# A two-layer trunk on one core: the order in which the down and output projections load their blocks

## The chip, the core and the metric

The kernel runs on one core of a Trainium2 chip. The core has a matrix engine (TensorE, PE in the profile; its weight loads are PEld), three engines for elementwise work (VectorE or DVE, ScalarE or ACT, GpSimd or POOL), and SyncE (SP), which here does nothing but issue transfers. ACT and POOL issue some transfers too. Each has a queue of instructions of its own. The metric is the time of one execution on the device in microseconds (us); lower is better.

## The reference, cut to what matters

A trunk of two layers over a sequence of 1024 rows of width 1024, all in float32. Each layer has a mixer, a layer norm, a convolutional feed-forward part and a second layer norm:

```python
for i in range(DEPTH):                      # DEPTH = 2
    ...
    y = mixers[i % N_MIXERS](x * (1.0 + sc1) + sh1)
    x = layer_norm(DN_ALPHA * x + (1.0 + g1) * y, ln_g[i, 0], ln_b[i, 0])
    y = conv_ffn(x * (1.0 + sc2) + sh2, ffn_up[i], ffn_conv_w[i], ffn_conv_b[i], ffn_down[i])
    x = layer_norm(DN_ALPHA * x + (1.0 + g2) * y, ln_g[i, 1], ln_b[i, 1])
```

Layer 0's mixer is a gated delta net, layer 1's is retention. The two that are never reached are left out. The change touches two matrix products:

```python
def conv_ffn(h, w_up, conv_w, conv_b, w_down):
    ...
    return (jax.nn.silu(gate) * up) @ w_down          # 1024 x 2816 by 2816 x 1024, once per layer
def retention(h, w_in, w_out):
    ...
    return o.astype(h.dtype) @ w_out                   # 1024 x 2048 by 2048 x 1024, layer 1
```

## The kernel before, in words

**Precision.** Every float32 operand of a large product is split in two parts of a reduced format, a high and a low one: `split` (line 88) copies the block into the high part on ACT and subtracts it on DVE for the low part. A product of two blocks is then three matmuls (low by high, high by low, high by high), lines 278 to 280 in `mma`.

**The projections.** `proj_gen` (line 1265) computes the down projection of each layer and the output projection of retention. It cuts the rows, the columns and the inner dimension into halves and uses a Strassen-Winograd scheme with seven block products instead of eight. The seven are listed in `prods` (line 1419); each names an activation operand (`11`, `12`, `22`, `S1` to `S4`), a weight operand (`11`, `21`, `22`, `T1` to `T4`) and a function that merges the result. A product has `nj` steps, 11 in the down projections and 8 in the output projection, so a projection has 77 or 56 steps. A step multiplies one activation block of 128x512 with one weight block of 128x512 into four PSUM banks: twelve matmuls.

**What a step loads.** The activation blocks were combined earlier (the sums S1 to S4 included) and stored in DRAM, `ad` for the down projections and `od` for the output projection; `ablk` (made by `ablk_of`, line 1258) takes a buffer called `ar` from the tag `qkv` and loads one of them on SP's queue (line 1261). The weight blocks are loaded by `load_b` (line 1284, the transfer on line 1294) and combined on the fly by `bblk` on DVE (lines 1302, 1305, 1307). The blocks `11` and `T2` stay for later products (`Bw`; line 1294 writes them to the tag in `slots`), the others are short-lived (`Br`, tag `qkv`). The operand `22` needs no load of its own: it is the block kept for `T2`. `ops` (line 1312) does one step: it loads the activation block, combines the weight block and splits both.

**Buffers.** The tag `qkv` has 24 buffers of 128x512. In the down projections the `ar`, the `Br` and, in eleven of them, the blocks of `T2` share them. In the output projection they are shared with the split values of the retention (`vv`, two buffers for each chunk of 128 rows of a head). The targets of the splits (`ab`, `bb`) come from other tags, except in the last steps.

**Order.** Three loops run over product, step and row group. `ahead = 3` (line 1424): three weight blocks are loaded before the first step, and step n, after its own activation block, loads the weight block of step n+3, with `after("a")` queueing it behind the last activation load. The rows that the down projection also needs are fetched in the same loop: `gain_half` (line 1335) loads a half row group `xg` behind the last load of a block, POOL multiplies and adds to it, and it is stored again; `xload` (line 1344) and `load_row` (line 269) load the residual rows `xt`, also behind the last block's load.

The output projection is interleaved by hand with the retention: `run` (line 647) draws from generators by their due times, and `gate(j)` (line 1434) holds back step j of the first two products until the retention has written the activation blocks of its head. `take` and `give` keep account of the buffers of `qkv` in this interleaving; 20 of the 24 are in that account.

What the program says is not yet the order of the queues. At compile time a scheduler plays the program through in a model of time, hands out the buffers of a tag in program order as they come free, and lays down the order of each engine's queue; an instruction is queued when its operands and its buffer are ready in that model. Edges such as those of `after` are kept. On the chip the queues then run in that fixed order.

Of the kernel before, what the change touches and what calls it, by code (L numbers as in the profile page):

```python
# [33 lines left out]
def trunk_kernel(ctx: ExitStack, tc, A):  # L34
# [14 lines left out]
    def two(tag, dt=F32, name=None):  # L49
        if tag in ("qkv", "auh"):  # L50
            return tl(tag, [P, HALF], dt, name), tl(tag, [P, HALF], dt, name)
        t = tl(tag, [P, 2, HALF], dt, name)
        return t[:, 0], t[:, 1]
# [13 lines left out]
    def acc4():  # L67
        return [acc_tile(), acc_tile(), acc_tile(), acc_tile()]
# [19 lines left out]
    def split(dst_h, dst_l, src, eng=dve):  # L88
        act.activation(dst_h, src, AF.Copy)  # L89
        eng.tensor_tensor(dst_l, src, dst_h, ALU.subtract)  # L90
# [3 lines left out]
    def after(key):  # L94
        return tc.issue_after(anchor[key].ins) if key in anchor else nullcontext()
# [23 lines left out]
    def bg_step(tile=mm_tile):  # L119
        bg_ps[0] = tile  # L120
        if bg:
            bg.pop(0)()
# [38 lines left out]
    for k in range(KT):  # L161
        w = two("hTa", F32, "mvw")
# [113 lines left out]
    def mma(acc, t, a, w, first, last, mm):  # L276
        sl = slice(t * P, (t + 1) * P)
        mm(acc, a[1][:, sl], w[0], start=first, stop=False)  # L278
        mm(acc, a[0][:, sl], w[1], start=False, stop=False)  # L279
        mm(acc, a[0][:, sl], w[0], start=False, stop=last)  # L280
# [108 lines left out]
    def ln_hooks(half, xts, tag, vecs2, out, dst, key, npool=0):  # L389
        def build(f):  # L390
            out.append(build_one(tag, xts, *vecs2(), f, pool if f < npool else dve))
        return ([lambda f=f: build(f) for f in range(KT)]
                + [lambda t=t: ln_store(half, t, xts, dst, key) for t in range(4)])
# [297 lines left out]
    def take(tag, n):  # L691
        while free[tag] < n:
            yield lambda: free[tag] >= n
        free[tag] -= n

    def give(tag, n):
        free[tag] += n
# [567 lines left out]
    def proj_gen(nj, ablk, wsrc, slots, xsrc, G, final, ln_next, tag, ltags, dst, key, mm=pe.matmul, gate=None, gain=None):  # L1265
# [18 lines left out]
        def load_b(bn, j):  # L1284
            if bn not in src:
                return
            if bn == "11":
                t = C[j] = keep("c", j)
            elif bn == "T2":
                t = X[j] = keep("x", j)  # L1290
            else:
                t = R[bn, j] = tl("qkv", [P, HALF], name="Br")
            m = src[bn]
            anchor["w"] = sp.dma_start(t, wsrc[(m[1] == "2") * 1, j][:, hs((m[0] == "2") * 1)])

        def bblk(bn, j):
            if bn in ("11", "22"):
                return {"11": C, "22": X}[bn][j]
            if bn == "21":
                return R[bn, j]  # L1300
            if bn == "T1":
                dve.tensor_tensor(C[j], R[bn, j], C[j], ALU.subtract)
                return C[j]
            if bn == "T2":
                dve.tensor_tensor(C[j], X[j], C[j], ALU.subtract)
                return C[j]
            dve.tensor_tensor(R[bn, j], C[j], R[bn, j], ALU.subtract)  # L1307
            return R[bn, j]

        nst = [0]  # L1310

        def ops(an, bn, j, early):
            ra, rb = ablk(an, j), bblk(bn, j)
            n = nst[0]
            nst[0] += 1
            last = an == "22"
            at = ltags[0] if last and j >= nj - ltags[3] else ("wl", "hTb", "wr")[n % 3] if early else ("wl", "wr")[n % 2]
            wt = ltags[1] if last and j >= nj - ltags[2] else ("wh", "hTb", "hTb")[n % 3] if early else "wh"
            a = two(at, F32R, "ab")
            split(a[0], a[1], ra, pool if j < bal[an] else dve)  # L1320
            w = two(wt, F32R, "bb")
            split(w[0], w[1], rb, pool if j < bal["w" + bn] else dve)
            return a, w
# [3 lines left out]
        def acc_next():  # L1327
            nacc[0] += 1
            return sc_tile() if nacc[0] % 6 in (5, 0) else acc_tile()
# [5 lines left out]
        def gain_half(n):  # L1335
            hf, rs = n // 4, slice(HALF + n % 4 * P, HALF + (n % 4 + 1) * P)
            x = tl("lane", [P, HALF], name="xg")
            with after("w"):
                sp.dma_start(x, gain[1][rs, hs(hf)])
            for r, op in zip(grows, (ALU.mult, ALU.add)):  # L1340
                pool.tensor_tensor(x, x, r[hf], op)
            pool.dma_start(xsrc[rs, hs(hf)], x)

        def xload(half, t):
            xt = load_row(xsrc if half or not gain else gain[1], half, t)
            if half == 0 and gain:
                for r, op in zip(grows, (ALU.mult, ALU.add)):
                    for hf in range(2):
                        pool.tensor_tensor(xt[:, hs(hf)], xt[:, hs(hf)], r[hf], op)
            xts[half].append(xt)  # L1350
            stats[half].append(tl("st", [P, 2, 6]))

        def finish(half, t, nh, c):
            dve.tensor_tensor(c, c, G[nh], ALU.mult)  # L1354
            xv = xts[half][t][:, hs(nh)]
            dve.scalar_tensor_tensor(xv, xv, ALPHA, c, ALU.mult, ALU.add)  # L1356
            dve.bn_stats(stats[half][t][:, nh], xv)  # L1357
# [55 lines left out]
        def f4(t, acc):  # L1413
# [5 lines left out]
        prods = [("11", "11", f1), ("12", "21", f2), ("S1", "T1", f5), ("S2", "T2", f6), ("S4", "22", f3),  # L1419
                 ("S3", "T3", f7), ("22", "T4", f4)]  # L1420
        if not gate:
            prods.insert(3, prods.pop(1))
        steps = [(bn, j) for _, bn, _ in prods for j in range(nj)]
        ahead = 3
        for st in steps[:ahead]:
            load_b(*st)
        hooks = []
        for p, (an, bn, fin) in enumerate(prods):
            accs = acc4() if gate and p < 2 else [acc_next() for _ in range(4)]
            tail = []  # L1430
            depth = ltags[3] if p == 6 else 2
            for j in range(nj):
                if gate and p < 2:
                    yield gate(j)
                    yield from take("qkv", 2)
                    give("qkv", 2)
                a, w = ops(an, bn, j, not gate and p < (7 if final else 5))
                with after("a"):
                    for st in steps[p * nj + j + ahead:p * nj + j + ahead + 1]:
                        load_b(*st)  # L1440
                if gain and p < 2 and j % 2 == 0 and p * 4 + j // 2 < 8 and j < 8:
                    gain_half(p * 4 + j // 2)
                if gain and p == 2 and j % 2 == 0 and j < 8:
                    xload(0, j // 2)
                if p == 2 and j < 4 and gate:
                    xload(0, j)
                    finish(0, j, 0, c11[j])
                if j >= nj - depth:
                    tail.append((j, a, w))
                else:  # L1450
                    for t in range(4):
                        mma(accs[t], t, a, w, j == 0, False, mm if p < 2 else pe.matmul)
                        yield 0.0
                if p == 5 and j > 1:
                    for _ in range(-(-16 // (nj - 2))):
                        if hooks:
                            hooks.pop(0)()
                bg_step()
            if p == 5:
                while hooks:  # L1460
                    hooks.pop(0)()
            if p == 6:
                pin[0] = None
            for t in range(4):
                for j, a, w in tail:
                    mma(accs[t], t, a, w, j == 0, j == nj - 1, mm if p < 2 else pm if p == 6 else pe.matmul)
                fin(t, accs[t])
                yield 0.0
            if p == 1:
                yield "P2"  # L1470
            if p == 4:
                hooks = [] if final else ln_hooks(0, xts[0], tag, ln_next, outs, dst, key, bal["h"])
                hooks += [lambda t=t: xload(1, t) for t in range(4)]
# [12 lines left out]
    def layer_tail(i, mix, wout, xsrc, x_mid, x_out, ln_next, final):  # L1486
# [23 lines left out]
        def pair_items(fp):  # L1510
# [31 lines left out]
            def up_start():  # L1542
                seen = []

                def gated(q, a, b):
# [7 lines left out]
                    if len(seen) == 4:  # L1553
# [9 lines left out]
        slots = {"c": "hTa", "x": "qkv"}  # L1563
        gb2 = gain_rows(3, ("mid", i), "hTb") if final else None
        return proj_st(proj_gen(NF // 2, ablk_of(ad, "qkv"), A["ffn_down"][i], slots, xg[i + 1], rows[i, 5],
                       (gb2, x_out) if final else None, ln_next, "hTb", ("hTb", "hTa", 8, 6, "f") if final else ("qkv", "hTa", 8, 4, "0"), x_out, ("out", i), gain=(2 * i, x_mid)))

# [354 lines left out]
```

## Time and profile before

| | |
|---|---|
| time before, median of 3 runs | 3033.51 us (3031.15 to 3038.18) |
| time of the profiled execution | 3032.61 us |
| its span, from the first to the last instruction | 3030.8 us |
| mean granted TensorE clock | 0.971 |
| first and last activation load of layer 0's down projection | 1201.9 and 1403.4 us |
| first and last activation load of the output projection | 2098.8 and 2285.9 us |
| first and last activation load of layer 1's down projection | 2767.8 and 2964.3 us |
| transfers `ar<-ad`, `ar<-od` | 154 and 56 of 256 KB |
| transfers `Br<-in_ffn_down`, `Bw<-in_ffn_down` | 88 and 44 of 256 KB |
| transfers `Br<-in_ret_wout`, `Bw<-in_ret_wout` | 32 and 16 of 256 KB |

In the profile "L1261" is line 1261 of the kernel, and `out<-in` names the tiles that an instruction writes and reads. "SPq" is the queue of transfers that SP issues; the duration beside such a row is that of issuing, and the landing comes later. A row of a timeline gives the start, the duration, the engine, the line and the operation, and in brackets how long the engine had been idle before it and what ended that. A row of waits reads "engine line <- what it waited for: total us, times, longest us". `L89` and `L90` are the two halves of a split: `ab` is the split of an activation block, `bb` that of a weight block. `acc` and `sc` are PSUM banks. The times of a row are microseconds from the start of the span, unless they are given as minimum/median/maximum, which are nanoseconds for instructions.

### The profile page before, as it was taken

What the parts mean: (1) busy time and instruction counts of PE and PEld (TensorE: products, weight loads), DVE (VectorE), ACT (ScalarE), POOL (GpSimd) and SP (SyncE); (2) the same over time, 40 slices, a digit from 0 to 9 for tenths busy, and PEclk for the clock granted to TensorE, in tenths of its full rate; (3) what the DMA queues carried; (4) which work ended last, traced back from release to release, by engine and by line L of the source; (5) the groups of instructions that cost most, each with busy time, mean ns of one, the idle gap of its engine ahead of it and who ended that gap; (6) DMA issues with size and microseconds to landing.
All of it is one profiled execution on the core that took longest, in us unless ns stands there. A gap on an engine that the chain in (4) does not pass through costs nothing. (4 is left out here: it accounts for less than half of the span.)

```text
span 3030.8 us, 38796 instructions
## 1 busy us (share of the span) xinstructions
PE 2840.2 (94%) x13590; PEld 2312.4 (76%) x13590; DVE 2271.4 (75%) x3841; ACT 1316.8 (43%) x2408; POOL 672.8 (22%) x629
## 2 busy tenths in 40 slices
PE   8889998999999999998999999999999899999997
PEld 7768876887778788786777787767777678888785
DVE  5785786545888888998788645566688887778988
ACT  4655555434544445445432442222243544445442
POOL 0410311033021111730023303422200011113704
PEclk9999998999999999999999999999998999999998
DMA  7222221354344545854322444666663332336663
GB/s 271 89 70 74 98 82 62 116 170 138 106 153 151 158 158 182 309 193 141 126 105 98 166 160 144 200 184 186 202 217 132 98 136 104 105 105 227 232 188 108
DMA packets 243027, 450.22 MB, mean 149 GB/s; under 512 B 22928, under 2 KB 76432, under 8 KB 242832
## 3 DMA queue, kind: packets, MB, share of 16 engines
q1 hardware_dynamic: 211648, 400.02, 40.0%
q10 hardware_dynamic: 29760, 43.00, 3.9%
q0 software_dynamic: 1424, 4.72, 0.4%
q8 instruction: 107, 1.75, 0.2%
q14 instruction: 88, 0.72, 0.1%
HBM read 339.13 MB, written 108.53 MB: 148 GB/s over the span
## 5 line engine op out<-in xcount | busy, mean ns | idle before, releaser
L636 PE MATMUL acc<-hT,wh 128*128 128x512 f32 x960 | 302.8, 397 | 0.0
L1556 POOL TENSOR_TENSOR o<-o 128x512 f32<-128x512 f32 x88 | 121.1, 1386 | 725.4 <-DVE o L1549 622.9
L279 PE MATMUL acc<-bb,ab 128*128 128x512 f32 x504 | 205.5, 408 | 18.8 <-DVE bb L90 18.7
L1158 PE MATMUL acc<-T,wb 128*128 128x512 f32 x840 | 205.3, 393 | 8.7 <-DVE wb L90 8.6
L636 PEld LDWEIGHTS acc<-hT,wh 128*128 128x128 f32 x960 | 184.3, 192 | 34.5
L278 PE MATMUL acc<-bb,ab 128*128 128x512 f32 x504 | 192.2, 407 | 16.9 <-DVE ab L90 10.3
L636 PE MATMUL acc<-hT,wl 128*128 128x512 f32 x480 | 204.3, 426 | 0.3 <-ACT sg L1084 0.3
L89 ACT ACTIVATE ab<-ar 128x512 fp32r<-128x512 f32 x210 | 129.8, 624 | 168.6 <-PE acc L280 87.9
L280 PE MATMUL acc<-bb,ab 128*128 128x512 f32 x504 | 202.6, 403 | 0.0
L1158 PEld LDWEIGHTS acc<-T,wb 128*128 128x128 f32 x840 | 157.9, 189 | 46.1 <-DVE wb L90 12.4
L90 DVE TENSOR_TENSOR wb<-wr,wb 128x512 fp32r<-128x512 f32 x162 | 116.0, 718 | 92.8 <-ACT wb L89 89.5
L90 DVE TENSOR_TENSOR ab<-ar,ab 128x512 fp32r<-128x512 f32 x210 | 169.2, 812 | 15.1 <-ACT ab L89 14.7
L90 DVE TENSOR_TENSOR wl<-wr,wh 128x1024 fp32r<-128x1024 f32 x85 | 106.4, 1252 | 89.7 <-ACT wh L89 89.7
L90 DVE TENSOR_TENSOR wb<-mm,wb 128x512 fp32r<-128x512 f32 x216 | 145.1, 683 | 22.8 <-ACT wb L89 20.9
L89 ACT ACTIVATE wh<-wr 128x1024 fp32r<-128x1024 f32 x101 | 106.8, 1058 | 121.3 <-PE acc L636 56.1
L89 ACT ACTIVATE wb<-mm 128x512 fp32r<-128x512 f32 x216 | 122.8, 593 | 72.5 <-DVE mm L1204 72.4
L1215 ACT ACTIVATE pc<-acc 128x512 f32<-128x512 f32 x143 | 84.5, 593 | 154.0 <-PE acc L1158 95.2
L636 PE MATMUL acc<-wh,hT 128*128 128x512 f32 x384 | 138.0, 422 | 2.0 <-DVE vv L90 2.0
L89 ACT ACTIVATE wb<-wr 128x512 fp32r<-128x512 f32 x162 | 99.3, 627 | 92.2 <-DMA wr<-in_ffn_up 45.9
L1535 DVE SCALAR_TENSOR_TENSOR o<-g,vc,o 128x512 f32<-128x512 f32 (+2 forms) x176 | 138.2, 804 | 0.8 <-ACT o L1530 0.2
L457 DVE SCALAR_TENSOR_TENSOR qkv<-raw,vc,qkv 128x512 f32<-128x512 f32 x144 | 114.6, 800 | 30.4 <-ACT qkv L455 29.3
L279 PEld LDWEIGHTS acc<-bb,ab 128*128 128x128 f32 x504 | 98.9, 196 | 44.7 <-DVE bb L90 24.3
(634 smaller groups left out, 7792.0 us busy)
## 6 DMA issues: line engine op xcount, KB each, us to landing
wr<-in_ffn_up SPq DMA_DIRECT2D x96, 512.0 KB, 4.0
mvw<-in_ada_w SPq DMA_DIRECT2D x80, 512.0 KB, 4.3
ad<-o SPq DMA_DIRECT2D x154, 256.0 KB, 2.2
ar<-ad SPq DMA_DIRECT2D x154, 256.0 KB, 4.4
Br<-in_ffn_down SPq DMA_DIRECT2D x88, 256.0 KB, 4.1
wr<-in_ret_wv SPq DMA_DIRECT2D x32, 512.0 KB, 3.7
ar<-od SPq DMA_DIRECT2D x56, 256.0 KB, 5.3
xs<-xt ACTq DMA_DIRECT2D x24, 512.0 KB, 3.8
```

What stands on the lines that cost most here:

```text
L89: act.activation(dst_h, src, AF.Copy)
L90: eng.tensor_tensor(dst_l, src, dst_h, ALU.subtract)
L278: mm(acc, a[1][:, sl], w[0], start=first, stop=False)
L279: mm(acc, a[0][:, sl], w[1], start=False, stop=False)
L280: mm(acc, a[0][:, sl], w[0], start=False, stop=last)
L457: dve.scalar_tensor_tensor(oh, raw[:, 3 - j:515 - j], w[:, 3 - j:4 - j], oh, ALU.mult, ALU.add)
L636: pq(pe.matmul(out, lhsT, rhs, start=start, stop=stop), cost)
L1158: return pe.matmul(*a, skip_group_check=True, **kw)
L1215: act.activation(t, X, AF.Copy)
L1535: dve.scalar_tensor_tensor(tv, gv[:, c0 - j:c1 - j], w[:, 2 - j:3 - j], tv, ALU.mult, ALU.add)
L1556: pool.tensor_tensor(o[d], o[x], o[y], op)
```

## The change

`ops` no longer loads its activation block. A new function `load_a(n)` loads the blocks of steps n, n+1 and n+2 as far as they are not loaded yet, and is called at the head of `ops` with the number of the step; the loaded blocks are kept in `araw`. In the gated projection (the output projection) a block of the first two products is only loaded in its own step, and from the third product on two steps ahead as well. `ahead` becomes 5: five weight blocks are loaded before the first step, and step n loads the weight block of step n+5. Everything else stays: the buffers, the splits, the matmuls and the merging functions.

```diff
         nst = [0]
 
-        def ops(an, bn, j, early):
-            ra, rb = ablk(an, j), bblk(bn, j)
+        araw = {}
+
+        def load_a(n):
+            for q in range(n, min(n + 3, 7 * nj)):
+                if q not in araw and not (gate and (q < 2 * nj or n < 2 * nj) and q > n):
+                    araw[q] = ablk(prods[q // nj][0], q % nj)
+
+        def ops(an, bn, j, early, at_step):
+            load_a(at_step)
+            ra, rb = araw[at_step], bblk(bn, j)
             n = nst[0]
...
-        ahead = 3
+        ahead = 5
         for st in steps[:ahead]:
             load_b(*st)
...
-                a, w = ops(an, bn, j, not gate and p < (7 if final else 5))
+                a, w = ops(an, bn, j, not gate and p < (7 if final else 5), p * nj + j)
                 with after("a"):
                     for st in steps[p * nj + j + ahead:p * nj + j + ahead + 1]:
                         load_b(*st)
```

## The prediction

> **What bounds the kernel now.** First the page: its span and its busy rows.
>
> ```profile
> span 3030.8 us, 38796 instructions
> ...
> PE 2840.2 (94%) x13590; PEld 2312.4 (76%) x13590; DVE 2271.4 (75%) x3841; ACT 1316.8 (43%) x2408; POOL 672.8 (22%) x629
> ```
>
> TensorE (PE) is busy for 94% of the span, so a change of loads can only be worth what PE idles in the stages that it touches. Next, therefore, the busy time by stage: the down projection of layer 0, the output projection of layer 1 with the end of the retention around it, and the down projection of layer 1. The first figure is the length, the second the time that PE is busy; then come PEld, DVE, ACT and POOL, the granted clock, the DMA share and GB/s.
>
> ```profile
> 1195.00:1435.00 240.00, 224.56 (x966) 181.49 (x965) 221.12 (x312) 117.63 (x210) 82.01 (x48) 0.96 0.64 219
> 2036.00:2330.00 294.00, 274.20 (x1163) 212.11 (x1162) 219.84 (x384) 102.01 (x179) 48.57 (x73) 0.95 0.58 187
> 2766.00:3031.00 265.00, 238.30 (x1007) 192.58 (x1006) 238.83 (x335) 108.20 (x189) 110.40 (x68) 0.95 0.59 201
> ```
>
> PE idles 15.4, 19.8 and 26.7 us there, 61.9 in all, and VectorE (DVE) is busy almost as long as PE: 221 and 239 us in the two down projections. Third, who waited for whom in the same three stretches (total, times, longest). PE's own waits, first in the two down projections:
>
> ```profile
> PE acc L279 <- DVE bb L90: 12.5, 5, 4.0
> ```
> ```profile
> PE acc L278 <- DVE ab L90: 7.2, 4, 2.9
> PE acc L279 <- DVE bb L90: 3.4, 2, 3.0
> ```
>
> PE never waits for a transfer; it waits for the second half of a split on DVE. So the question is whether the splits wait for transfers. For ACT (first half of a split) and DVE, with layer 0's down projection in the first fence, the output projection in the second, layer 1's down projection in the third:
>
> ```profile
> DVE Br L1307 <- DMA Br<-in_ffn_down: 13.5, 11, 3.4
> ...
> ACT ab L89 <- DMA ar<-ad: 4.3, 3, 1.9
> ```
> ```profile
> ACT ab L89 <- DMA ar<-od: 10.8, 3, 5.6
> ...
> DVE Br L1307 <- DMA Br<-in_ret_wout: 3.6, 3, 1.6
> ```
> ```profile
> DVE Br L1307 <- DMA Br<-in_ffn_down: 4.8, 5, 2.5
> ...
> ACT ab L89 <- PE acc L280: 59.9, 26, 14.6
> ...
> ACT ab L89 <- DMA ar<-ad: 6.0, 5, 2.0
> ```
>
> ACT waits 21.1 us for activation blocks and DVE 21.9 us for weight blocks. In the last stage ACT waits ten times as long, 59.9 against 6.0 us, for PE to give a split's target buffer back. A block that lands earlier does not shorten that wait.
>
> **How early the blocks are issued already.** Issue on SP's queue and first use on ACT, for the first step of layer 0's down projection and for step 66 (which loads and which splits these are is counted in order of time):
>
> ```profile
> 1201.90 0.44 SPq L1261 DMA_DIRECT2D ar<-ad  x1
> ...
> 1368.77 0.32 SPq L1261 DMA_DIRECT2D ar<-ad  x1
> ```
> ```profile
> 1210.24 0.63 ACT L89 ACTIVATE ab<-ar 128x512 fp32r<-128x512 f32 x1
> ...
> 1403.81 0.61 ACT L89 ACTIVATE ab<-ar 128x512 fp32r<-128x512 f32 x1
> ```
> ```profile
> L90 DVE TENSOR_TENSOR ab<-ar,ab x210: 635/683/5970, 1212.4 to 3002.9; 128x512 fp32r<-128x512 f32 x105
> L1261 SPq DMA_DIRECT2D ar<-ad x154: 319/320/1491, 1201.9 to 2964.3; - x154
> L1261 SPq DMA_DIRECT2D ar<-od x56: 319/320/565, 2098.8 to 2285.9; - x56
> ...
> DMA to landing us min/median/max: 2.4/4.9/8.0
> ```
>
> The lead is 8.3 us at the start and 35.0 us later, against 4.9 us from issue to landing. One step costs PE about 2.8 us (twelve matmuls; 966 took 224.56 us). So an activation block that the program loads in the step that uses it is in fact issued 3 to 12 steps before, in the queue that the scheduler lays down. What holds the loads back is seen in the waits of SP's own queue in layer 0:
>
> ```profile
> SPq L1294 <- DVE ab L90: 37.5, 24, 8.6
> SPq L1261 <- DVE bb L90: 32.4, 25, 5.4
> ```
>
> A load waits for a split to give up one of the 24 qkv buffers. The buffers set the distance, not the place of the load in the program.
>
> **The change part by part.** No instruction is added or removed: the same 210 activation loads and the same weight loads are issued, at 0.32 us each on SP's queue, so the bill for issuing is 0.
>
> Weight blocks two steps earlier and activation blocks two steps earlier, in the down projections: before, the order was ar(n), B(n+3); now it is ar(n+2), B(n+5). Block B(k+3) still stands right behind ar(k), and the two still share the 24 buffers in that order. From the third step on I therefore expect the same queue: 0 us. Above, if the distance grew after all, it could be worth the one place where a late weight block reached PE:
>
> ```profile
> 1372.29 0.33 SPq L1294 DMA_DIRECT2D Br<-in_ffn_down  x1
> ```
> ```profile
> 1374.99 0.69 DVE L1307 TENSOR_TENSOR Br<-Bw,Br 128x512 f32<-128x512 f32 x1 [2.12 <-DMA Br<-in_ffn_down]
> ```
> ```profile
> 1382.32 0.50 PE L279 MATMUL acc<-bb,ab 128*128 128x512 f32 x1 [3.13 <-DVE bb L90]
> ```
>
> DVE, in order, stood 2.12 us for a weight block that it combines about ten steps early, and the splits behind it came late. Bound: a gain of 3.1 us.
>
> The start of each projection: five weight blocks instead of three stand ahead of ar(0), two issues of 0.33 us, 0.7 us. The cover is ar(0)'s slack, 8.3 us of lead less 4.9 to land, 3.4 us. I take 0; without the cover it is 0.7 us a projection.
>
> Other transfers hang behind the moved ones. The helper rows (xg, line 1339) and the residual rows (xt, line 273) are queued behind the last weight load traced, so they now stand behind B(n+5) instead of B(n+3). In layer 1 the second xg load and the weight load that it must now follow:
>
> ```profile
> 2772.55 0.32 SPq L1339 DMA_DIRECT2D xg<-xs  x1
> ...
> 2778.65 0.43 SPq L1294 DMA_DIRECT2D Bw<-in_ffn_down  x1
> ```
>
> It moves by 6.5 us. POOL multiplies these rows, and nothing on PE waits for them soon; but POOL and DVE hinder one another:
>
> ```profile
> 2800.11 3.02 POOL L1341 TENSOR_TENSOR xg<-xg,rowb 128x512 f32<-128x512 f32 x2
> ```
> ```profile
> 2803.60 5.97 DVE L90 TENSOR_TENSOR ab<-ar,ab 128x512 fp32r<-128x512 f32 x1
> ```
> ```profile
> 2809.71 0.47 PE L278 MATMUL acc<-bb,ab 128*128 128x512 f32 x1 [2.86 <-DVE ab L90]
> ```
>
> A split whose median is 0.68 us took 5.97 us, and PE stood 2.86 us. Moving POOL's work can remove that stall or make another. The same number of POOL operations falls on equally dense DVE work, so I take 0, with 2.9 us either way for each of the two down projections, 5.8 us.
>
> The output projection: in its first two products only the block of the step itself is loaded, since the retention writes the blocks meanwhile, so here the weight blocks do go two further ahead of the activation blocks. No PE wait there hangs on a weight block; ACT's 10.8 us are for activation blocks, which do not move. From the third product on it is as in the down projections. I take 0; the bound above is under the rivals, below it the 3.6 us that DVE waits for weight blocks.
>
> Sum: 0 + 0 + 0 + 0 = 0 us on the profiled execution's 3030.8 us of span and 1.8 us around it, 3032.6 us, which is 0.9 us under the median of 3033.5 us. Forecast: the median again, 3033.5 us. Its own range, from the 5.8 us either way, is 3027.7 to 3039.3.
>
> **The rivals.** *The weight blocks take the buffers of the retention (slower).* Place: SP's queue around 2118 us.
>
> ```profile
> SPq L1758 <- DVE kz L1691: 21.4, 2, 11.7
> ```
> ```profile
> 2108.97 1.52 PE L636 MATMUL sc<-vv,kz 128*128 128x512 f32 x6
> 2117.97 1.52 PE L636 MATMUL sc<-vv,kz 128*128 128x512 f32 x6
> ```
>
> By count, six activation blocks, one weight block and 12 to 16 value tiles of head 3 hold 19 to 23 of the 24 buffers then; two more weight blocks make 21 to 25. Over 24, a weight load waits in SP's queue until the retention ends a step, 9.0 us apart, and the gate loads (line 1758) that the retention needs queue behind it, as they already do for 11.7 us. It decides from one buffer too many: 9 us for one such wait, 18 for two, so 3042 to 3052. For it: the count comes to the edge. Against: the queue order is planned with the buffers in it, so such a load should be placed behind the gate loads.
>
> *The order of DVE and POOL changes for the worse (slower).* The scheduler lays all queues anew; a collision of 2.9 us in each projection, and one more in the output projection, give 3033.5 + 8.7 = 3042. For it: DVE is busy 221 of 240 us. Against: no compute instruction has moved in the program. The Trainium skill's page "SBUF — State Buffer", "Who interferes with whom", says that a two-input DVE operation and a reading GpSimd operation lock each other out for a whole instruction; the 5.97 us agree, and by it, too, a shifted POOL operation must hit some split.
>
> *The loads do run further ahead (faster).* The largest wait of PE in the output projection comes at the start of its third product, whose blocks are loaded late:
>
> ```profile
> PE acc L278 <- DVE ab L90: 3.2, 1, 3.2
> ```
>
> Gain: 3.1 us of the late weight block, 2.9 us for each of two collisions gone, and these 3.2 us: 12.1 us, so 3021.4. For it: 43.0 us of waits for transfers on ACT and DVE. Against: the buffers. The Trainium skill's page "Trainium Kernel Development and Optimization", "Best Practices", asks for transfers overlapped with compute; this trace has that already, and a lead of 35.0 us over 4.9 us leaves that rule nothing to gain.
>
> **How the numbers follow.** What a measurement of this kernel can tell from no change is about 0.2%, 6.1 us. My forecast, that the change hardly does what it says, has 0.49; the buffers of the retention 0.12 and the worse order 0.18, both slower by over 6.1 us; the loads further ahead 0.21. So faster 0.21, same 0.49, slower 0.30. The range reaches to 3021 on the fast side, the whole of that rival, and to 3050 on the slow side, most of both.
>
> **What would show it.** Right: the leads stay at about 8 and 35 us, SP's queue keeps B(k+3) behind ar(k), and PE's idle time in the three stretches stays within 3 us each. Wrong: an SP wait of about 9 us on a Br load near 2118 us with gate loads behind it; a DVE split of over 3 us in a new place with PE idle after it; or ACT's and DVE's 43.0 us for transfers halved and PE's idle time with them.

## The result, and the profile after

| | before | after |
|---|---|---|
| median of 8 runs each | 3035.85 us (3022.47 to 3042.60) | 3053.36 us (3046.58 to 3062.95) |
| ratio after/before | | 1.006, 95% interval 1.0039 to 1.0081 |
| profiled execution, and its span | 3032.61 us, 3030.8 us | 3054.45 us, 3052.7 us |

The change costs 17.5 us, 0.6%. The forecast was no change at all.

The first question is where. The blocks' first matmul (line 278) marks both ends of a down projection. The view of a line gives the start of its first and last matmul; first row layer 0, second row layer 1. Before:

```profile
L278 PE MATMUL acc<-bb,ab x204: 387/389/796, 1217.0 to 1444.3; 128*128 128x512 f32 x102
...
L278 PE MATMUL acc<-bb,ab x196: 387/389/766, 2784.8 to 3001.3; 128*128 128x512 f32 x196
```

After:

```profile
L278 PE MATMUL acc<-bb,ab x204: 387/390/795, 1222.8 to 1457.6; 128*128 128x512 f32 x102
...
L278 PE MATMUL acc<-bb,ab x196: 388/389/628, 2800.3 to 3023.2; 128*128 128x512 f32 x196
```

Layer 0's down projection grew from 227.3 to 234.8 us, layer 1's from 216.5 to 222.9: 7.5 and 6.4, together 13.9 us. The other 5.8 us by which the first matmul of layer 0 starts later lie ahead of the first changed transfer. No part of the change reaches them: up to there PE, DVE, POOL and SP carry out the same instructions in the same order in both kernels. In the executions below this start varies from 1216.5 to 1231.2 us. The output projection, from its first matmul to its last, takes 211.29 us before (2123.34 to 2334.63) and 212.55 after (2134.88 to 2347.43), 1.3 us more.

The second question is who made PE wait. PE's waits after, layer 0 in the first fence, layer 1 in the second (total, times, longest):

```profile
PE acc L279 <- DVE bb L90: 12.9, 8, 4.1
PE acc L278 <- DVE xt L1364: 4.0, 2, 3.0
PE sc L278 <- DVE xt L1364: 2.9, 1, 2.9
PE acc L278 <- DVE ab L90: 1.3, 1, 1.3
```
```profile
PE acc L279 <- DVE bb L90: 13.2, 2, 12.8
PE acc L278 <- DVE ab L90: 4.9, 5, 2.0
PE acc L636 <- DVE ab L90: 1.9, 1, 1.9
PE acc L278 <- DVE xt L1364: 0.7, 1, 0.7
```

The sums are 21.1 us in layer 0 and 20.7 in layer 1. Before they were 15.4 (12.5, and 1.5 and 1.4 behind `xt` operations) and 12.9 (7.2, 3.4, and two of 1.6 and 0.7). In layer 1 one single wait of 12.8 us stands where the longest was 3.0. In layer 0 the loss is in several small ones. The place of the long one, on POOL, DVE and PE in turn (timeline: start, duration, engine, line, operation; in brackets the idle time before and what ended it):

```profile
2828.37 25.79 POOL L1349 TENSOR_TENSOR xg<-xg,rowb 128x512 f32<-128x512 f32 x2 [5.64 <-DMA xg<-xs]
...
2862.29 0.58 POOL L1350 DMA_DIRECT2D xg<-xg  x1 [0.30 <-POOL xg L1349]
2862.89 19.73 POOL L1357 TENSOR_TENSOR xt<-xt,rowb 128x512 f32<-128x512 f32 x16
```
```profile
2860.76 1.78 DVE L90 TENSOR_TENSOR ab<-ar,ab 128x512 fp32r<-128x512 f32 x1
2862.46 20.72 DVE L90 TENSOR_TENSOR bb<-Bw,bb 128x512 fp32r<-128x512 f32 x1
2883.10 0.68 DVE L90 TENSOR_TENSOR ab<-ar,ab 128x512 fp32r<-128x512 f32 x1
```
```profile
2883.23 0.80 PE L279 MATMUL acc<-bb,ab 128*128 128x512 f32 x1 [12.82 <-DVE bb L90]
```

POOL does the 16 gain operations on the residual rows `xt` (four rows, two operations by two halves each) back to back, 1.23 us each. A split that alone takes 0.68 us is held on DVE all that time, 20.72 us. PE works off the splits made ahead and then stands for 12.82 us. Before, the same 16 operations fell in two runs of eight (here with the held operation on DVE and PE's wait behind it):

```profile
2817.64 19.47 POOL L1341 TENSOR_TENSOR xg<-xg,rowb 128x512 f32<-128x512 f32 x2 [7.75 <-DMA xg<-xs]
...
2841.32 0.58 POOL L1342 DMA_DIRECT2D xg<-xg  x1 [0.30 <-POOL xg L1341]
2841.93 10.01 POOL L1349 TENSOR_TENSOR xt<-xt,rowb 128x512 f32<-128x512 f32 x8
2858.55 17.23 POOL L1349 TENSOR_TENSOR xt<-xt,rowb 128x512 f32<-128x512 f32 x8 [6.61 <-DMA xt<-xs]
```
```profile
2841.50 10.99 DVE L1305 TENSOR_TENSOR Bw<-Bw 128x512 f32<-128x512 f32 x1
```
```profile
2853.15 0.50 PE L279 MATMUL acc<-bb,ab 128*128 128x512 f32 x1 [2.96 <-DVE bb L90]
```

The first eight hold DVE for 10.99 us and cost PE 2.96. The second eight take 17.23 us: the first of them takes 5.33 us, until just after DVE had a gap of 0.98 us, the other seven 1.74 us each. There POOL and DVE take turns, and no operation of DVE lasts over 1.78 us.

The run of 16 carries layer 1. Matched matmul by matmul, with the first set equal, the changed kernel is 8.3 us ahead of the kernel before just ahead of the long wait, 4.7 us behind it right after, and 6.4 us behind at the end.

Why eight before and sixteen after is read on SP's queue. Before, and then after; between them the row of SP's waits before, from 2838 to 2870 us:

```profile
2831.40 0.32 SPq L273 DMA_DIRECT2D xt<-xs  x1
...
2841.60 0.33 SPq L1294 DMA_DIRECT2D Br<-in_ffn_down  x1
2854.33 0.32 SPq L1261 DMA_DIRECT2D ar<-ad  x1
2854.75 0.37 SPq L273 DMA_DIRECT2D xt<-xs  x1
```
```profile
SPq L1261 <- DVE ab L90: 17.7, 5, 12.3
```
```profile
2857.93 0.32 SPq L273 DMA_DIRECT2D xt<-xs  x1
2858.34 0.38 SPq L1261 DMA_DIRECT2D ar<-ad  x1
2858.82 0.38 SPq L1294 DMA_DIRECT2D Br<-in_ffn_down  x1
2862.57 0.32 SPq L1261 DMA_DIRECT2D ar<-ad  x1
2863.37 2.43 SPq L273 DMA_DIRECT2D xt<-xs  x2
```

Before, an activation load stood between the second and the third `xt` load. It waits for a buffer that DVE must free, DVE was held, and so SP stood from 2841.60 to 2854.33 us. The third row came late, POOL ran dry after eight operations, and its hold on DVE ended by itself. After, the third and fourth `xt` loads go out together at 2863.37 us, ahead of the next block load. POOL never runs dry and the hold lasts for all 16 operations.

Layer 0 is another matter. There POOL's run has seven operations and holds a split for 9.74 us, but no wait of PE follows. It waits at 1246 us and then not again until 1359, when POOL's last `xt` operation has been over for 38 us (1321.55). POOL, DVE and PE after:

```profile
1287.25 8.76 POOL L1357 TENSOR_TENSOR xt<-xt,rowb 128x512 f32<-128x512 f32 x7
```
```profile
1286.82 9.74 DVE L90 TENSOR_TENSOR bb<-Bw,bb 128x512 fp32r<-128x512 f32 x1
```
```profile
1246.12 0.80 PE L279 MATMUL acc<-bb,ab 128*128 128x512 f32 x1 [4.05 <-DVE bb L90]
...
1359.38 0.50 PE L278 MATMUL acc<-bb,ab 128*128 128x512 f32 x1 [1.00 <-DVE xt L1364]
```

Matched in the same way, layer 0 is 2.2 us behind at 1349 us and loses the other 5.3 us after that. This late loss is followed up below; the run of seven does not explain it.

### The profile page after: what moved, and what is told of

The parts are those of the page before. It is cut to its first block, busy times and chain, and to the rows that moved or that the text cites. A ratio compares the mean times of both kernels' runs of the same rounds, so it can differ in the third digit from the quotient of the medians.

```text
span 3052.7 us, 38794 instructions
## 1 busy us (share of the span) xinstructions
PE 2847.0 (93%) x13590; PEld 2316.4 (76%) x13590; DVE 2276.8 (75%) x3841; ACT 1316.6 (43%) x2408; POOL 675.4 (22%) x629
## 5 line engine op out<-in xcount | busy, mean ns | idle before, releaser
L90 DVE TENSOR_TENSOR ab<-ar,ab 128x512 fp32r<-128x512 f32 x210 | 161.7, 778 | 21.4 <-ACT ab L89 21.3
L90 DVE TENSOR_TENSOR bb<-Bw,bb 128x512 fp32r<-128x512 f32 x120 | 129.6, 1088 | 8.9 <-ACT bb L89 8.8
```

## The experiments

Four theories were put to the test. Theory 1: the look-ahead of the blocks does nothing; the loss comes from the `xg` and `xt` loads that it pushed behind `B(n+5)`, and so from where POOL's gain operations fall against DVE. Theory 2: the depth of the weight blocks costs, through the shared buffers. Theory 3: the depth of the activation blocks costs. Theory 4: chance of newly laid queues. In the diffs "two steps" are steps of the projection. The ratio of each run is to the kernel before, on the same chip; it is not the quotient of the two medians given with it and differs from that by up to 0.001.

**1. `xearly`: the change, with the `xg` and `xt` loads where they were.**

```diff
+                if gain:
+                    n = p * nj + j
+                    for m in range(n + 2 if n else 0, n + 3):
+                        pq, jq = divmod(m, nj)
+                        if jq % 2 == 0 and jq < 8:
+                            if pq < 2 and pq * 4 + jq // 2 < 8:
+                                gain_load(pq * 4 + jq // 2)
+                            elif pq == 2:
+                                xt0[jq // 2] = load_row(gain[1], 0, jq // 2)
```

Here `gain_load` is the load of `gain_half` by itself; the operations and the store stay in their step.

> The changed kernel, with the loads of the rows xg and xt of the two down projections called two steps earlier in the program, so that they stand behind B(n+3) again as in the kernel before; weight and activation blocks as far ahead as in the change. Theory 1 (the look-ahead of the blocks does nothing; the loss comes from the xg and xt loads that were pushed behind B(n+5), so that POOL's gain operations fall elsewhere against DVE): the loss of 17.5 us goes, ratio to before 1.000 (0.998 to 1.002), and in layer 1 no run of 16 gain operations on xt back to back with a DVE split of 20 us under it. Theory 2 (the look-ahead of the blocks itself costs, through the shared buffers): ratio stays near 1.006. Theory 4 (chance of a new queue order anywhere): anything from 0.997 to 1.006.

Measured: 3036.83 against 3034.33 us, ratio 1.0003 (0.9990 to 1.0016). The loss is gone with both look-aheads in place: as explanations of the 0.6% theories 2 and 3 fall. POOL's runs in layer 1 are 7 and 9 operations. What does not go is the late loss of layer 0: in `xearly` this projection loses 4.0 us behind 1341 us against the kernel before, where the change loses 5.3 (one profiled execution each). So that part does not come from where the `xg` and `xt` loads stand, and "the look-ahead does nothing" is not true of layer 0; the interval leaves room for up to 0.16%, 4.9 us.

**2. `xlate`: the kernel before, with only those loads and their operations two steps later.**

```diff
-                if gain and p < 2 and j % 2 == 0 and p * 4 + j // 2 < 8 and j < 8:
-                    gain_half(p * 4 + j // 2)
+                pq, jq = divmod(p * nj + j - 2, nj)
+                if gain and 0 <= pq < 2 and jq % 2 == 0 and jq < 8:
+                    gain_half(pq * 4 + jq // 2)
...
```

> The kernel before, with nothing changed but that the xg and xt loads of the down projections and their gain operations are called two steps later in the program; weight blocks three steps ahead, activation blocks in their own step. Theory 1: slower like the changed kernel, ratio 1.004 to 1.008, with POOL's gain operations on xt in layer 1 in one run of 16 of about 20 us, a DVE split held for as long, and PE idle 10 us or more after it. Theories 2 and 3 (the look-ahead of the weight or activation blocks itself costs): ratio 1.000, within 0.002. Theory 4: anything.

Measured: 3047.43 against 3034.33 us, ratio 1.0041 (1.0025 to 1.0056). Without the longer look-ahead a loss of this size is there, at the lower end of what was expected, and its picture in layer 1 is that of the change, first POOL, then DVE, then PE's wait:

```profile
2854.47 19.73 POOL L1349 TENSOR_TENSOR xt<-xt,rowb 128x512 f32<-128x512 f32 x16
```
```profile
2854.04 20.71 DVE L90 TENSOR_TENSOR bb<-Bw,bb 128x512 fp32r<-128x512 f32 x1
```
```profile
PE acc L279 <- DVE bb L90: 13.2, 2, 12.8
```

In layer 0 the picture is not that of the change: POOL has a run of 11, PE waits 5.34 us for it at 1302.51 us, and nothing is lost behind 1354 us.

**3 and 4. `w5` and `a2`: each half of the change alone.** `w5` is the kernel before with `ahead = 5`; `a2` is the changed kernel with `ahead = 3`.

> The kernel before with ahead = 5 alone: weight blocks five steps ahead, activation blocks in their own step. Theory 1: the xg and xt loads stand behind B(n+5) here too, so about 1.004 to 1.007. Theory 2 (depth of the weight blocks): 1.006. Theory 3 (depth of the activation blocks): 1.000. Theory 4: anything from 0.997 to 1.006.

> The changed kernel with ahead = 3: activation blocks two steps ahead, weight blocks three. Theory 1: the xg and xt loads stand behind ar(n+2) here, pushed back by about as much as in the change, so 1.003 to 1.007. Theory 2 (depth of the weight blocks): 1.000. Theory 3 (depth of the activation blocks): 1.006. Theory 4: anything from 0.997 to 1.006.

Measured: `w5` 3048.51 us, 1.0049 (1.0033 to 1.0064); `a2` 3039.06 us, 1.0019 (1.0005 to 1.0033), both against 3034.33. For `a2` theory 1 had expected 1.003 to 1.007, too much: the loads moved, but in layer 1 the third `xt` load again stands behind an activation load that is held, POOL's runs are 7 and 9, and that projection is even shorter than before. So "pushed back by two steps" is not the cause by itself; in layer 1 the loss goes with the length of the run. `w5` has a run of 16 in both layers. In layer 0:

```profile
1288.80 19.76 POOL L1349 TENSOR_TENSOR xt<-xt,rowb 128x512 f32<-128x512 f32 x16
```
```profile
1309.26 0.76 PE L278 MATMUL acc<-bb,ab 128*128 128x512 f32 x1 [12.21 <-DVE ab L90]
```

**5 and 6. `nog_b` and `nog_a`: both kernels without the gain operations on `xg` and `xt`.**

```diff
-            for r, op in zip(grows, (ALU.mult, ALU.add)):
-                pool.tensor_tensor(x, x, r[hf], op)
             pool.dma_start(xsrc[rs, hs(hf)], x)
...
-                        pool.tensor_tensor(xt[:, hs(hf)], xt[:, hs(hf)], r[hf], op)
```

> The kernel before without POOL's gain operations on xg and xt in both down projections: the multiplication by the gain row and the addition of the bias row are left out; the loads and the stores of these rows stay. It gives the price of these operations in the kernel before. Theory 1: DVE is no longer held off, so part of PE's 15.4 and 26.7 us of idle time in the two stretches goes: ratio to before 0.992 to 0.998. Rival (the loss has nothing to do with POOL): 1.000.

> The changed kernel without the same gain operations on xg and xt (left out as in nog_b). Theory 1: the 0.4 to 0.6% by which the change is slower is gone, and this one lies within 0.2% of nog_b. Rival (look-ahead, buffers or another queue order): it stays 0.4% or more above nog_b.

Measured, against 3035.84 us: `nog_b` 3017.18 us, 0.9942 (0.9927 to 0.9957); `nog_a` 3018.51 us, 0.9945 (0.9929 to 0.9960). Without POOL's operations the change is worth nothing that can be measured either way, and in the kernel before these operations cost 18.7 us.

**7 to 10. The operations on DVE.** `xtdve_b` and `xtdve_a` move those on `xt` to DVE, `alldve_b` and `alldve_a` those on `xg` too:

```diff
-                        pool.tensor_tensor(xt[:, hs(hf)], xt[:, hs(hf)], r[hf], op)
+                        dve.tensor_tensor(xt[:, hs(hf)], xt[:, hs(hf)], r[hf], op)
```

> The kernel before with the 16 gain operations on xt of each down projection on DVE in place of POOL (xg stays on POOL). On DVE they take about 0.69 us each like the other subtractions of 128x512, 11 us in all, in place of 16 POOL operations of 1.23 us that hold DVE off for up to 19.7 us. Theory 1: no DVE operation of over 8 us near 2840 to 2880 us, ratio to before 0.995 to 1.001. Rival (DVE is full at 239 of 265 us, so that 11 us more per projection cost more than the holds): 1.003 to 1.007.

> The changed kernel with the same 16 gain operations on DVE. Theory 1: the long run on POOL is gone, so it lies within 0.2% of xtdve_b. Rival (look-ahead, buffers, queue order): 0.4 to 0.6% above xtdve_b.

> The kernel before with the gain operations on xt and on xg of both down projections on DVE: 32 more operations of about 0.69 us per projection, 22 us on a DVE that is busy 221 of 240 and 239 of 265 us, part of it with holds. Theory 1 (a POOL operation costs DVE more than the same work done on DVE itself): ratio to before 0.993 to 0.999, at or below the 0.9975 of xtdve_b. Rival (DVE becomes the bound): 1.001 to 1.006.

> The changed kernel with the same operations on DVE. Theory 1: within 0.2% of alldve_b. If the look-ahead were worth something by itself, it would show here, where POOL no longer disturbs: below alldve_b by more than 0.2%.

Measured: `xtdve_b` 3026.57 us, 0.9975 (0.9961 to 0.9990) and `xtdve_a` 3030.61 us, 0.9981 (0.9969 to 0.9993), against 3035.84; `alldve_b` 3018.36 us, 0.9940 (0.9925 to 0.9956) and `alldve_a` 3017.95 us, 0.9939 (0.9923 to 0.9955), against 3035.38. Each pair agrees: in the whole time the look-ahead has no worth of its own that can be measured. The rival that DVE is too full is refuted, and `alldve_b` and `alldve_a` are 17 us faster than the kernel before, as fast as leaving the operations out. The busy rows say why; first `nog_b`, then `alldve_b` with its two groups on DVE (count, busy us, mean ns):

```profile
PE 2826.5 (94%) x13590; PEld 2303.7 (76%) x13590; DVE 2208.1 (73%) x3841; ACT 1316.6 (44%) x2408; POOL 543.2 (18%) x565
```
```profile
PE 2829.4 (94%) x13590; PEld 2305.5 (76%) x13590; DVE 2235.0 (74%) x3905; ACT 1317.5 (44%) x2408; POOL 571.4 (19%) x565
```
```profile
L1341 DVE TENSOR_TENSOR xg<-xg,rowb 128x512 f32<-128x512 f32 x32 | 22.5, 710 | 0.1
L1349 DVE TENSOR_TENSOR xt<-xt,rowb 128x512 f32<-128x512 f32 x32 | 20.8, 691 | 0.5 <-DMA xt<-xs 0.5
```

The 64 operations take 22.5 + 20.8 = 43.3 us on DVE. On POOL they had lengthened DVE's own operations by 2271.4 - 2208.1 = 63.3 us. DVE as a whole is busy only 2235.0 - 2208.1 = 26.9 us longer in `alldve_b` than in `nog_b`. Work taken off the busy engine cost it more than doing it.

**11. `xgdve_a`: the change with the operations on `xg` alone on DVE.** The edit is that of `alldve_a` for the line of `xg` only.

> The changed kernel with the gain operations on xg alone on DVE; those on xt stay on POOL. Theory 1a (the run of 16 on xt comes from POOL's backlog: two xg operations starve for 25.8 us while all xt loads land): POOL takes each xt as it lands, in runs of 4 to 8, and the ratio is 0.996 to 1.001. Theory 1b (the run of 16 comes from the loads alone, which land together): the run of 16 and a DVE hold of about 20 us stay, ratio 1.002 to 1.006.

Measured: 3034.68 against 3035.38 us, 0.9993 (0.9979 to 1.0006). The time is that of theory 1a, but the runs on `xt` are not broken up. They are 16 long, and yet no split is held for long:

```profile
2855.23 29.84 POOL L1357 TENSOR_TENSOR xt<-xt,rowb 128x512 f32<-128x512 f32 x16 [3.21 <-DMA xt<-xs]
```
```profile
2858.91 1.21 DVE L90 TENSOR_TENSOR ab<-ar,ab 128x512 fp32r<-128x512 f32 x1 [0.49 <-ACT ab L89]
2860.04 1.77 DVE L90 TENSOR_TENSOR bb<-Bw,bb 128x512 fp32r<-128x512 f32 x1
```

POOL takes 1.87 us for each operation on average instead of 1.23 and DVE's splits 1.77 us: the two take turns. Both the reason of 1a (shorter runs) and that of 1b (a long run must hold DVE) fail. Turns are not free either: `alldve_a`, which differs only in having the `xt` operations on DVE too, is 16.7 us faster. But they make no long hold.

**12. `space_a`: the change with the `xt` loads three steps apart in the program.**

```diff
-                if gain and p == 2 and j % 2 == 0 and j < 8:
-                    xload(0, j // 2)
+                if gain and p == 2 and j % 3 == 0:
+                    xload(0, j // 3)
```

> The changed kernel with the four xt loads three steps apart in the program instead of two. Theory 1a (backlog): the last load comes after POOL has freed itself, so the run of 16 in layer 1 breaks in two, ratio 0.999 to 1.003. Rival (where a run falls against DVE's work decides, not its length): no better than the change, 1.004 to 1.007.

Measured: 3054.64 against 3035.38 us, 1.0054 (1.0040 to 1.0068): no better than the change. The theory of spacing fell, and POOL's run in layer 1 is 16 again. SP's queue still has the last two `xt` loads next to each other, at 2860.61 us, ahead of a weight load that only goes out at 2881.19:

```profile
2860.61 2.53 SPq L273 DMA_DIRECT2D xt<-xs  x2
2881.19 0.33 SPq L1294 DMA_DIRECT2D Br<-in_ffn_down  x1
```

All of it in one table. The lengths are from the first to the last matmul of line 278 on `acc`, as above, one profiled execution each; the difference of medians is to the kernel before measured next to it.

| kernel | layer 0, us | layer 1, us | both, to before | POOL's long run without turns, layer 0 / layer 1 | difference of medians, us |
|---|---|---|---|---|---|
| before | 227.3 | 216.5 | 0 | none / 8 | 0 |
| after | 234.8 | 222.9 | +13.9 | 7 / 16 | +17.5 |
| `xearly` | 231.5 | 216.8 | +4.5 | none / 7 | +2.5 |
| `xlate` | 234.7 | 223.9 | +14.8 | 11 / 16 | +13.1 |
| `w5` | 237.7 | 220.4 | +14.3 | 16 / 16 | +14.2 |
| `a2` | 230.4 | 211.4 | -2.0 | 6 / 7 | +4.7 |
| `space_a` | 233.0 | 225.6 | +14.8 | 7 / 16 | +19.3 |
| `xgdve_a` | 230.4 | 210.0 | -3.4 | none / none | -0.7 |
| `xtdve_b`, `xtdve_a` | 225.7, 229.5 | 214.4, 210.1 | -3.7, -4.2 | none | -9.3, -5.2 |
| `alldve_b`, `alldve_a` | 222.7, 225.5 | 206.6, 207.8 | -14.5, -10.5 | none | -17.0, -17.4 |
| `nog_b`, `nog_a` | 218.1, 220.0 | 207.0, 205.5 | -18.7, -18.3 | none | -18.7, -17.3 |

The four kernels with a run of 16 without turns are the four that are slower by 13 us or more. Layer 1's length follows the run. Layer 0's does not: `after` and `space_a` with 7 and `xlate` with 11 are about equal. Matched against the kernel before from 1341 us of its time on, four kernels lose 3.7 to 6.8 us: `after` 5.3, `xearly` 4.0, `space_a` 3.7, `xgdve_a` 6.8. They are the four that have both halves of the look-ahead and the `xt` operations on POOL; the nine others lie between -1.7 and +1.3. In `after` and `xearly` DVE waits there for weight blocks (1.49 us at 1406.79 and 2.00 at 1414.43; 2.66 at 1397.19 and 2.00 at 1404.84; in the kernel before 0.96 at 1395.32). What makes this late loss was not tested and stays open.

## Why the prediction was wrong, step by step

- **"A change of loads can only be worth what PE idles in the stages that it touches."** That bounds a gain, and it was used as if it bounded the loss as well. PE's waits grew by 7.8 us in layer 1 and by 5.7 in layer 0.
- **Weight and activation blocks earlier: 0 us, the buffers set the distance.** Right for the order and the distance, and for the time but for layer 0. On SP's queue `B(k+3)` still stands right behind `ar(k)`, and the leads are 7.7 us at the first step (load 1209.39, split 1217.13) and 36.5 at step 66 (1379.68, 1416.22), against 8.3 and 35.0 before. The waits of ACT and DVE for transfers are 45.0 us in the three stretches (17.6 and 9.5 in layer 0; 4.3, 3.1 and 1.3 in the output projection; 3.6 and 5.6 in layer 1), against 43.0. That sum hides a shift: in layer 0 they grew from 17.8 to 27.1, in the output projection they fell from 14.4 to 8.7. In the whole time `alldve_a` against `alldve_b` and `nog_a` against `nog_b` agree with the 0: 0.9939 and 0.9940, 0.9945 and 0.9942. In layer 0 the term was some 4 us too small, by the profile of `xearly`.
- **The start of each projection: 0.** Right in layer 0: from the first weight load to the first matmul it is 18.2 us before (1198.80 to 1217.0) and 18.3 after (1204.55 to 1222.8). It was not tested alone.
- **"Other transfers hang behind the moved ones ... I take 0, with 2.9 us either way for each of the two down projections."** This is the step that failed. The move was seen, the collision of POOL and DVE too, but its price was taken from one collision, 5.97 us on DVE and 2.86 on PE, and that one was misread. The POOL row shown with it (2800.11 us, 3.02 us long) is over at 2803.13, before the split starts at 2803.60. Under the split POOL ran four operations back to back, behind an issue:

```profile
2803.42 0.58 POOL L1342 DMA_DIRECT2D xg<-xg  x1 [0.30 <-POOL xg L1341]
2804.02 1.31 POOL L1556 TENSOR_TENSOR o<-o 128x512 f32<-128x512 f32 x1
2805.28 1.29 POOL L1341 TENSOR_TENSOR xg<-xg,rowb 128x512 f32<-128x512 f32 x1
2806.54 1.26 POOL L1556 TENSOR_TENSOR o<-o 128x512 f32<-128x512 f32 x1
2807.76 1.25 POOL L1341 TENSOR_TENSOR xg<-xg,rowb 128x512 f32<-128x512 f32 x1
```

So the collision that was priced was itself a run, and its price was that of four operations. The trace of before has a larger one that was not read: the run of eight above, with 10.99 us on DVE. Nor was it asked what ends such a run. It ends when the next `xt` row is late, and the rows' loads are what the change moves. The worst case was therefore in reach: 16 x 1.23 = 19.7 us of hold instead of 10.0, by estimate some 10 us more on PE for each projection. Measured were 12.82 us of waiting where 2.96 stood, while the 2.86 us of the collision that was priced went away. `xearly` shows that this step carries most of the loss: with these loads back in place the difference of medians falls from 17.5 to 2.5 us. `xlate` shows that moving them alone makes a loss of that kind. In layer 1 the wait behind the run makes the loss; in layer 0 the 5.3 us behind 1349 us stay unexplained.
- **"The same number of POOL operations falls on equally dense DVE work."** True, and beside the point: their grouping decides. In layer 1, 16 in a row make PE wait 12.8 us at once; with 16 in turns (`xgdve_a`) no wait of PE there is over 2.5 us.
- **The output projection: 0.** Nearly right, +1.3 us. The rival of the retention's buffers did not come: SP's wait at the gate loads is 21.0 us, against 21.4 before.

```profile
SPq L1766 <- DVE kz L1699: 21.0, 2, 11.1
```

- **The rival "the order of DVE and POOL changes for the worse", 3042 us, chance 0.18.** In layer 1 this is what happened, and its sign came too: a DVE split of over 3 us in a new place with PE idle after it (20.72 and 12.82 us). It had the mechanism and too small a price, three collisions of 2.9 us. The Trainium skill's page "SBUF — State Buffer", "Who interferes with whom", says that a DVE operation with two inputs in SBUF contends with a GpSimd operation that reads SBUF, and that the order of issue decides who blocks. The trace agrees that the two contend, and not on the rest: the split started at 2862.46 us, ahead of POOL's first operation at 2862.89, and was held for all 16. Nor do the 5.97 us agree with a lock of one operation, as the prediction has it.

The change does do what it says in the program, and the forecast was right that the block loads keep their order on SP's queue. What it did not price is what else stands in the same queue.

## What to carry to other kernels

When loads are moved, follow the other loads that hang on the same queue to the engine that uses them, and ask what sets the length of its runs: here the late row was a brake that kept POOL off DVE. Price a collision by the longest one in the trace, and by what would end it, not by a typical one. Elementwise work put on GpSimd beside a busy VectorE can cost VectorE more than doing it there: 63.3 against 43.3 us here, and the kernel with it on VectorE is the fastest complete one, 3018 us.

## What the runs showed of the hardware that was not expected

POOL and DVE meet in two ways. Either they take turns, 1.74 us for nearly every operation of POOL after a first one of 1.5 to 7.1 us, and no DVE operation lasts over 1.8 us; or POOL runs through at 1.23 to 1.26 us and holds one DVE operation for the whole run (10.99 us for 8, 20.72 us for 16). The runs of over 4 us on `xt` in the eight profiles with these operations on POOL sort without exception: all 12 that run through begin within 0.1 us behind POOL's own issue of the store of `xg`, and all 11 that take turns begin behind a wait. In all 12 of the first kind DVE's held operation starts during that issue (after the change at 2862.46 us, with the issue from 2862.29 to 2862.87). The issue alone does not decide: the pairs of operations on `xg` stand behind one too, and there DVE is held for the first of the two only (in the kernel before 2.28 us from 2837.59, under the pair that starts at 2838.01). What makes the difference was not tried.

It goes the other way too: two `xg` operations of POOL took 25.79 us after the change, while DVE worked back to back at 0.60 us from one split to the next. POOL got through once DVE had a gap of 0.54 us, waiting for ACT.
